# Sums of normalised activations for the seven-product multiplication: from GpSimd to VectorE

## The chip, the core and the metric

The kernel runs on one core of a Trainium2 chip. The metric is the device time of one execution in microseconds (us). In the profile PE is TensorE's matmuls, PEld its weight loads, DVE is VectorE, ACT is ScalarE, POOL is GpSimd and SP the engine that issues most of the DMAs.

## The reference

A decoder trunk of two residual layers over x of 512 tokens by 1024 features, in fp32, with a final norm. Each layer has an attention part and then a gated feed-forward part with a causal convolution of width 3. The change lies in the feed-forward part, which runs in both layers:

```
h = rmsnorm(x, ffn_norm[layer])            # x * rsqrt(mean(x*x) + 1e-6) * g
a, b = jnp.split(h @ w_in, 2, axis=-1)     # 1024 -> 2 x 2816
a = causal_conv3(a, conv_w) + conv_b
x = x + (jax.nn.silu(a) * b) @ w_out       # 2816 -> 1024
```

## The kernel before

Everything is kept transposed: features on the 128 partitions, 512 tokens along the free axis. X has 8 such tiles (NK = 8). To keep fp32 accuracy each operand is split in a high part (a cast to fp32r, by ACT) and a low part (the rest, by DVE), and a product is three matmuls: high x high, low x high, high x low. The names end in h or hi and l or lo (whi/wlo, xh/xl, sxh/sxl, gh/gl, b1h/b1l, t3h/t3l and so on).

`ffn(layer, nl, final)` computes the 22 chunks c of 128 hidden features. For each, a and b need 1024 x 128 weights times X. The first six chunks (PLAIN = 6) are done directly by `plain`: two units of 24 matmuls on 512 columns. They use x that is scaled by g but not yet by rstd; rstd is multiplied in at the evacuation, so that PE can start before the norm is known. The other sixteen chunks (`seven`) use a 2 x 2 block multiplication with seven products instead of eight, with the two halves of the tokens (LO, HI) and the two halves of the features (k and k + H, H = 4) as the blocks. That needs sums of blocks of the weights (`total`: p1, p2 and p4 on DVE, p3 on GpSimd) and sums of blocks of the normalised activations. The latter are made once per layer by `sums(k)` for k = 0 to 3, after rstd (root) is known, while PE works on the plain chunks. `sums(k)` does, in order: x[k] and x[k + 4] normalised on DVE; then four operations on half tiles of 128x256, s1 to s4, which fill d1 and d3 (two halves each); then the split of four operands into high and low parts, b1, b2, t1 (from d1) and t3 (from d3), a cast on ACT and a subtraction on DVE each. The last of these jobs, for all four k, are the list TJ, and every one of the seven products waits for all of TJ. In the profile x[k] has the tile name gh, and d1 and d3 have the name gl, because they are taken from the same buffers as the gated results GH and GL; the token "g" counts these ten buffers.

The outputs (`out(m, p)`) multiply the gated chunks of part p (PARTS: chunks 0 to 5, 6 to 11, 12 to 16, 17 to 21) with w_out for each of 8 tiles m and add to X[m].

The order of work on every engine is not written by hand: `add` gives a job to `Plan` with an engine, a planned cost, its dependencies, a priority (lower goes first) and buffer tokens that it takes and gives. `Plan.run` simulates the engines with these costs, picks at each step the job that can start first (priority decides among those that are ready), and emits the instructions in that order; each engine then works through its instructions in just that order. Priorities around the change: evacuations 1, convolution and gate 1.1, weight parts 1.2, weights of the outputs 1.3, `sums` 2 + 0.1 k; on PE, plain units and seven products 100 + c, outputs 200 + p. So the planned cost and the engine of one job can move the order of all that comes after it within the same feed-forward layer. Both layers get their own plan from the same code. Nearly all instructions carry line 88, the helper that records the order.

Of the kernel before, what the change touches and what calls it, by code (L numbers as in the profile page):

```python
# [39 lines left out]
class Fill:  # L40
# [5 lines left out]
    def add(self, *gens):  # L46
        self.q.extend([g, False] for g in gens)
# [122 lines left out]
def trunk(ctx, tc, A):  # L170
    nc = tc.nc
    inorder = [False]
    pe, act, dve, pool, sp = [Ordered(tc, e, inorder, e is nc.sync)
                              for e in (nc.tensor, nc.scalar, nc.vector, nc.gpsimd, nc.sync)]
# [946 lines left out]
    def ffn(layer, nl, final):  # L1121
# [7 lines left out]
        with ExitStack() as es:  # L1129
# [14 lines left out]
            def g_tile(t, dt=F32R):  # L1144
                return fp.tile([P, SEQ], dt, tag=t, bufs=10, name=t)

            def split(h, l, x, n, prio, *deps, take=(), give=()):

                j = add("ACT", 0.19 + 0.00085 * n, lambda: act.copy(h(), x()), *deps, prio=prio, take=take)
                return add("DVE", 0.16 + 0.00104 * n, lambda: dve.tensor_sub(l(), x(), h().bitcast(F32)), j, prio=prio, give=give)  # L1150
# [88 lines left out]
            def sums(k, root):  # L1239

                x = {}

                def norm(c):
                    x[c] = g_tile("gh", F32)
                    dve.scalar_tensor_tensor(x[c], X[c], ng[:, nl - 1, c:c + 1], rstd, op0=ALU.mult, op1=ALU.mult)
                    if c >= H:
                        x["d1"], x["d3"] = g_tile("gl", F32), g_tile("gl", F32)
                p = 2 + 0.1 * k
                j = add("DVE", 0.75, lambda: norm(k), root[0], prio=p, take=("g",))
                j = add("DVE", 0.75, lambda: norm(k + H), j, prio=p, take=("g",))  # L1250
                eng, e, cost = (pool, "POOL", 0.74) if True else (dve, "DVE", 0.42)
                s1 = add(e, cost, lambda: eng.tensor_sub(x["d1"][:, LO], x[k][:, LO], x[k][:, HI]), j, prio=p)
                s2 = add(e, cost, lambda: eng.tensor_add(x["d1"][:, HI], x[k + H][:, HI], x["d1"][:, LO]), s1, prio=p)
                s3 = add(e, cost, lambda: eng.tensor_sub(x["d3"][:, LO], x[k + H][:, HI], x[k][:, HI]), s2, prio=p)
                s4 = add(e, cost, lambda: eng.tensor_sub(x["d3"][:, HI], x["d1"][:, HI], x[k + H][:, LO]), s3, prio=p)
                part = lambda n, i: (lambda: B[n][i][:, k])
                a = split(part("b1", 0), part("b1", 1), lambda: x[k][:, LO], W, p, j, s4)
                b = split(part("b2", 0), part("b2", 1), lambda: x[k + H], SEQ, p, j, s4, give=("g",))
                c = split(part("t1", 0), part("t1", 1), lambda: x["d1"], SEQ, p, s2, s4)
                d = split(part("t3", 0), part("t3", 1), lambda: x["d3"], SEQ, p, s4, c, b, give=("g",))  # L1260
                TJ.extend((a, b, c, d))
# [137 lines left out]
            for c in range(PLAIN):  # L1399
                plain(c, root)  # L1400
                if c == 0:
                    for k in range(H):
                        sums(k, root)
# [277 lines left out]
```

## Time and profile before

| what | value |
|---|---|
| median of 3 runs | 1250.48 us (1249.95 to 1252.03) |
| the profiled execution | 1250.37 us, of which the span 1248.2 us |
| granted TensorE clock, mean | 0.995 |
| feed-forward part of the first layer | about 290 to 650 us of the span: plain chunks to 360.4, seven products to 611.9 |
| feed-forward part of the second layer | about 882 us to the end: plain chunks to 951.4, seven products to 1203 |

The span runs from the first to the last instruction in the trace of one execution; times in rows are us from its start unless marked ns. A matmul's shown duration overlaps with the next one's, so its cost is the step from one start to the next.

### The profile page before, as it was taken

The numbers are of one execution on the slowest core, as the hardware profiler recorded it, in microseconds if no ns is written. First come the engines' busy times: TensorE is split into PE (matmuls) and PEld (weight loads), VectorE is DVE, ScalarE is ACT, GpSimd is POOL, SyncE is SP. The second block draws the span as 40 slices with busy tenths as digits, with TensorE's granted clock in tenths as the row PEclk, the third lists the DMA queues.
The fourth block names the chain that finished last, engine by engine and source line by source line (L and its number), as shares of the span: only waits on it lengthen the run. The fifth ranks groups of instructions, "written<-read, shape, count | busy, mean of one in ns | idle before, by whom it ended". The sixth has DMA issues, their size and how long they took to land.

```text
span 1248.2 us, 19483 instructions
## 1 busy us (share of the span) xinstructions
PE 1223.1 (98%) x7484; PEld 1038.2 (83%) x7484; DVE 923.0 (74%) x1576; ACT 631.6 (51%) x1148; POOL 230.2 (18%) x272
## 2 busy tenths in 40 slices
PE   8999999999999999999999999999999999999997
PEld 5887866677889999999887878777788999999986
DVE  6668757658998799888762443444899889988875
ACT  6676537745554445444452664542555445444452
POOL 0000104413510001000030452310441000100011
PEclk9999999999999999999999999999999999999999
DMA  6314141012251342323233553312225124232421
GB/s 213 118 35 124 52 130 52 18 51 83 86 169 41 113 132 81 114 72 137 78 109 105 188 160 98 110 52 85 85 86 168 64 94 148 72 108 82 131 66 68
DMA packets 51420, 124.18 MB, mean 99 GB/s; under 512 B 6064, under 2 KB 17584, under 8 KB 51328
## 3 DMA queue, kind: packets, MB, share of 16 engines
q1 hardware_dynamic: 49808, 121.35, 30.0%
q10 hardware_dynamic: 1520, 1.59, 0.4%
q8 instruction: 59, 0.97, 0.3%
q14 instruction: 33, 0.27, 0.1%
HBM read 119.28 MB, written 2.13 MB: 97 GB/s over the span
## 4 chain that ended last, share of the span: by engine, by line
PE 88%; DVE 6%; ACT 1%; issue 1%; SPq 1%; DMA 1%; POOL 1%; DVEq 0%; ACTq 0%; POOLq 0%
PE mm L88 50%; PE s L88 20%; PE t L88 10%; PE o L88 7%; SPq L88 1%; DVE x L88 1%; DVE xl L88 1%; DVE wlo L88 1%; POOL e L88 1%; DVE e L88 1%; ACT whi L88 0%; DMA x<-x 0%; DVE sxl L88 0%; ACT xh L88 0%; DMA swp<-q 0%
## 5 line engine op out<-in xcount | busy, mean ns | idle before, releaser
L88 PE MATMUL mm<-xl,whi 128*128 128x512 f32 x424 | 166.2, 392 | 5.0 <-DVE xl L88 4.9
L88 PE MATMUL mm<-xh,whi 128*128 128x512 f32 x424 | 169.5, 400 | 1.4 <-ACT xh L88 1.4
L88 PE MATMUL mm<-xh,wlo 128*128 128x512 f32 x424 | 165.7, 391 | 1.1 <-DVE wlo L88 1.1
L88 DVE TENSOR_TENSOR wlo<-wraw,whi 128x1024 fp32r<-128x1024 f32 (+3 forms) x83 | 105.8, 1275 | 55.0 <-ACT whi L88 54.7
L88 ACT CAST whi<-wraw 128x1024 fp32r<-128x1024 f32 (+3 forms) x83 | 83.8, 1010 | 99.3 <-PE mm L88 73.8
L88 POOL TENSOR_TENSOR sr<-wraw,wb 128x512 f32<-128x512 f32 x32 | 47.4, 1481 | 462.8 <-DVE sr L88 288.1
L88 PE MATMUL mm<-gh,wlo 128*128 128x512 f32 x332 | 130.1, 392 | 0.0
L88 PE MATMUL mm<-gh,whi 128*128 128x512 f32 x332 | 130.0, 392 | 0.0
L88 PE MATMUL mm<-gl,whi 128*128 128x512 f32 x332 | 129.2, 389 | 0.0
L88 ACT CAST sxh<-sr 128x512 fp32r<-128x512 f32 x128 | 76.4, 617 | 83.5 <-DVE sr L88 54.2
L88 DVE TENSOR_TENSOR x<-x,mm 128x512 f32<-128x512 f32 (+2 forms) x104 | 70.0, 674 | 63.9 <-PE mm L88 63.5
L88 PEld LDWEIGHTS mm<-xl,whi 128*128 128x128 f32 x424 | 79.8, 188 | 24.6 <-DVE xl L88 7.5
L88 POOL TENSOR_SCALAR e<-e,dn 128x128 f32<-128x128 f32 (+3 forms) x128 | 72.3, 586 | 148.7 <-DVE dn L88 148.6
L88 PEld LDWEIGHTS mm<-xh,whi 128*128 128x128 f32 x424 | 79.9, 189 | 21.4 <-issue 3.3
L88 DVE TENSOR_TENSOR sxl<-sr,sxh 128x512 fp32r<-128x512 f32 x128 | 95.0, 760 | 2.7 <-ACT sxh L88 1.9
L88 PEld LDWEIGHTS mm<-xh,wlo 128*128 128x128 f32 x424 | 80.0, 189 | 18.1 <-DVE wlo L88 1.7
L88 ACT ACTIVATE tt<-a,conv 128x512 f32<-128x512 f32 x44 | 36.0, 817 | 114.5 <-DVE a L88 114.5
L88 ACT ACTIVATE e<-e,nm 128x256 f32<-128x256 f32 (+3 forms) x128 | 70.8, 556 | 43.9 <-DVE nm L88 40.9
L88 DVE SCALAR_TENSOR_TENSOR tt<-a,conv,tt 128x510 f32<-128x510 f32 x88 | 72.6, 826 | 8.4 <-ACT tt L88 7.2
L88 PEld LDWEIGHTS mm<-gl,whi 128*128 128x128 f32 x332 | 62.4, 188 | 13.3
L88 PE MATMUL s<-t3l,sxh 128*128 128x256 f32 x256 | 72.4, 283 | 0.0
L88 PE MATMUL s<-t3h,sxl 128*128 128x256 f32 x256 | 72.4, 283 | 0.0
(248 smaller groups left out, 3372.4 us busy)
## 6 DMA issues: line engine op xcount, KB each, us to landing
wraw<-wfi SPq DMA_DIRECT2D x56, 512.0 KB
wb<-wfi SPq DMA_DIRECT2D x32, 512.0 KB
wraw<-wu SPq DMA_DIRECT2D x31, 512.0 KB
wo<-wfo SPq DMA_DIRECT2D x32, 384.0 KB
wo<-wfo SPq DMA_DIRECT2D x28, 320.0 KB
wraw<-wo SPq DMA_DIRECT2D x16, 512.0 KB
wraw<-wv SPq DMA_DIRECT2D x10, 512.0 KB
cb<-cd SPq DMA_DIRECT2D x8, 512.0 KB
```

The lines of the kernel that those rows point to most:

```text
L88: r = f(*a, **k)
```

## The change

The engine variable that makes s1 to s4 in `sums` is GpSimd before and VectorE after; the planned cost of one goes from 0.74 to 0.42 us. The four operations, their operands, their dependencies and their priority stay. The function runs for four k in each of two layers, so 32 operations change their engine.

```
-                eng, e, cost = (pool, "POOL", 0.74) if True else (dve, "DVE", 0.42)
+                eng, e, cost = dve, "DVE", 0.42
                 s1 = add(e, cost, lambda: eng.tensor_sub(x["d1"][:, LO], x[k][:, LO], x[k][:, HI]), j, prio=p)
                 s2 = add(e, cost, lambda: eng.tensor_add(x["d1"][:, HI], x[k + H][:, HI], x["d1"][:, LO]), s1, prio=p)
                 s3 = add(e, cost, lambda: eng.tensor_sub(x["d3"][:, LO], x[k + H][:, HI], x[k][:, HI]), s2, prio=p)
```

The fourth operation, `s4`, follows in the same form.

## Rows read from the trace of the kernel before

**Rows 1.** The page: busy time, share of the span and instructions of each engine.
```profile
PE 1223.1 (98%) x7484; PEld 1038.2 (83%) x7484; DVE 923.0 (74%) x1576; ACT 631.6 (51%) x1148; POOL 230.2 (18%) x272
```

**Rows 2.** Windows: length, busy PE, PEld, DVE, ACT, POOL (instructions), clock, DMA share, GB/s.
```profile
290.00:360.38 70.38, 67.94 (x290) 55.02 (x289) 65.47 (x83) 38.17 (x57) 24.90 (x20) 0.98 0.33 109
360.38:611.90 251.52, 250.98 (x1736) 234.37 (x1735) 219.50 (x360) 115.14 (x195) 23.70 (x16) 1.00 0.30 99
...
882.10:951.37 69.27, 66.83 (x292) 54.18 (x290) 65.70 (x83) 38.25 (x57) 25.11 (x20) 1.00 0.34 111
951.37:1203.00 251.63, 251.39 (x1737) 234.61 (x1736) 220.13 (x362) 115.83 (x197) 23.70 (x16) 1.00 0.29 97
```

**Rows 3.** What PE waited for, whole span: us in total, times, longest us.
```profile
PE mm L88 <- DVE xl L88: 4.9, 2, 2.4
...
PE o L88 <- DVE sxl L88: 0.4, 1, 0.4
```

**Rows 4.** Groups by form on POOL, whole span: busy us, mean ns, idle before.
```profile
L88 POOL TENSOR_TENSOR gl<-gh 128x256 f32<-128x256 f32 x16 | 22.9, 1433 | 18.1 <-DVE gh L88 18.1
...
L88 POOL TENSOR_TENSOR gl<-gl,gh 128x256 f32<-128x256 f32 x8 | 10.6, 1319 | 0.0
L88 POOL TENSOR_TENSOR gl<-gh,gl 128x256 f32<-128x256 f32 x8 | 8.3, 1037 | 46.3 <-DVE gh L88 46.3
```

**Rows 5.** Timeline of POOL in the first layer: start us, duration us.
```profile
305.79 0.74 POOL L88 TENSOR_TENSOR gl<-gh 128x256 f32<-128x256 f32 x1 [9.47 <-DVE gh L88]
...
324.16 2.38 POOL L88 TENSOR_TENSOR gl<-gh 128x256 f32<-128x256 f32 x1
```

**Rows 6.** Groups by form on DVE between 304.3 and 357.25 us.
```profile
L88 DVE TENSOR_TENSOR wlo<-wraw,whi 128x1024 fp32r<-128x1024 f32 x9 | 11.7, 1303 | 0.0
...
L88 DVE SCALAR_TENSOR_TENSOR tt<-a,conv,tt 128x510 f32<-128x510 f32 x5 | 5.6, 1128 | 0.0
L88 DVE SCALAR_TENSOR_TENSOR tt<-a,conv,tt 128x511 f32<-128x511 f32 x5 | 5.2, 1037 | 0.2
...
L88 DVE TENSOR_TENSOR b1l<-gh,b1h 128x256 fp32r<-128x256 f32 x4 | 2.7, 684 | 0.0
```

**Rows 7.** Timeline of DVE in the first layer's plain stretch.
```profile
302.85 0.69 DVE L88 SCALAR_TENSOR_TENSOR rs_u<-rs_t,rs_u 128x512 f32<-128x512 f32 x1
303.58 0.69 DVE L88 SCALAR_TENSOR_TENSOR rstd<-rs_u,rstd 128x512 f32<-128x512 f32 x1
...
306.74 1.53 DVE L88 SCALAR_TENSOR_TENSOR tt<-a,conv,tt 128x510 f32<-128x510 f32 x2
...
317.53 0.41 DVE L88 TENSOR_TENSOR b1l<-gh,b1h 128x256 fp32r<-128x256 f32 x1
317.87 0.68 DVE L88 TENSOR_TENSOR b2l<-gh,b2h 128x512 fp32r<-128x512 f32 x1
318.47 0.68 DVE L88 TENSOR_TENSOR b<-mm,rstd 128x512 f32<-128x512 f32 x1
...
325.86 2.38 DVE L88 SCALAR_TENSOR_TENSOR tt<-a,conv,tt 128x510 f32<-128x510 f32 x2
...
342.80 1.22 DVE L88 TENSOR_TENSOR wlo<-wraw,whi 128x1024 fp32r<-128x1024 f32 x1
...
356.54 0.68 DVE L88 TENSOR_TENSOR t3l<-gl,t3h 128x512 fp32r<-128x512 f32 x1
```

**Rows 8.** Timeline of PE: a plain unit's first matmul, and the first of the seven products.
```profile
344.01 0.39 PE L88 MATMUL mm<-xh,whi 128*128 128x512 f32 x1
...
360.38 0.28 PE L88 MATMUL s<-b1h,sxh 128*128 128x256 f32 x1
```

**Rows 9.** Timeline of DVE in the second layer: the last part made from the sums.
```profile
947.60 0.68 DVE L88 TENSOR_TENSOR t3l<-gl,t3h 128x512 fp32r<-128x512 f32 x1
```

**Rows 10.** The chain that ended last, in order of time: start us, us, what.
```profile
398.85 15.67 PE mm L88 x69
```

**Rows 11.** Windows, the 10 us in that block; columns as in rows 2.
```profile
400.00:410.00 10.00, 10.00 (x46) 8.29 (x45) 6.83 (x10) 3.87 (x6) 0.00 (x0) 1.00 0.51 184
```

More of the change, by code (lines that the diff above doesn't have):

```diff
@@ L1250, in sums @@
                 j = add("DVE", 0.75, lambda: norm(k + H), j, prio=p, take=("g",))
-                eng, e, cost = (pool, "POOL", 0.74) if True else (dve, "DVE", 0.42)
+                eng, e, cost = dve, "DVE", 0.42
                 s1 = add(e, cost, lambda: eng.tensor_sub(x["d1"][:, LO], x[k][:, LO], x[k][:, HI]), j, prio=p)
```

## The prediction

> **What bounds the kernel now.** I read the profile from the whole to the place of the change. The busy line comes first: PE is busy for 1223.1 of the 1248.2 us of span, DVE 74%, POOL 18% [rows 1]. The cut by stages says the same of both feed-forward layers: in the stretch with the plain products PE is busy for 67.94 of 70.38 us, in the stretch of the seven products for 250.98 of 251.52, and the second layer repeats it with 66.83 of 69.27 and 251.39 of 251.63 [rows 2]. In the plain stretch DVE is almost as full (65.47 of 70.38), so both engines have to be watched. The list of what PE waited for names what is not covered: 4.9 us in two waits for xl, and 0.4 us for sxl [rows 3]. The xl wait lies before rstd exists, and no sum can start before rstd, so this change cannot touch it. What is left for it to win is the missing PE time of the two later stretches: 251.52 - 250.98 = 0.54 and 251.63 - 251.39 = 0.24 us [rows 2], together 0.8 us or 0.06% of the time. So the question is only whether the change makes PE wait.
>
> **What is removed.** 32 GpSimd instructions on 128x256 tiles, 16 in each layer: in the trace d1 and d3 are called gl and the x tiles gh. They took 22.9 + 10.6 + 8.3 = 41.8 us in all [rows 4]. GpSimd sits idle around them, so its own time buys nothing. What matters is what they do to DVE. The first of them, run with little DVE work beside it, took 0.74 us; another took 2.38 [rows 5]. DVE's instructions beside them are stretched too: a pair of convolution taps took 1.53 us in one place and 2.38 beside the sums, b1l 0.41 and 0.68 on average [rows 6, 7]. I price this from the means of the plain stretch, against an undisturbed one: taps 5 x (1.128 - 0.75) + 5 x (1.037 - 0.75) = 3.3 us, b1l 4 x (0.684 - 0.41) = 1.1, wlo 9 x (1.303 - 1.22) = 0.75 [rows 6, 7], where 0.75 is about half of the undisturbed pair and 1.22 a wlo with no sum beside it. That is 5.2 us of DVE given back in each layer. Bounds: nothing if the stretching has another cause, 5.2 if all of it is GpSimd's. I take 5.2, because the stretched rows lie exactly where a sum runs.
>
> The Trainium skill, page "SBUF — State Buffer", section "Who interferes with whom", says that a DVE instruction with two SBUF inputs and a GpSimd instruction that reads SBUF take an exclusive lock, so that the later one is fully blocked. Taken to its end, each of the 16 sums would hold DVE off for its whole 0.74 us, an estimate of 11.8 us per layer instead of the 5.2 of the rows; DVE would then come out 5.9 us lighter, not heavier, and the wait of the first rival below could not arise. The trace agrees in kind (both sides of an overlapping pair are lengthened) but not in that amount.
>
> **What is added.** The same 32 operations on DVE. A 256-column fp32 subtraction there is busy for 0.41 us, but the next instruction starts 0.34 us after it (317.53 to 317.87); at 512 columns the step is 0.60 (317.87 to 318.47), and 0.73 where the next one reads the result (302.85 to 303.58), 0.13 more [rows 7]. In a group of four only the second reads what the one before it wrote, so a group costs 4 x 0.34 + 0.13 = 1.49 us and four groups 6.0 us per layer. Bounds: 16 x 0.34 = 5.4 (others in between) and 16 x 0.47 = 7.5 (all dependent). Net on DVE: 6.0 - 5.2 = +0.8 us per layer, between +0.2 (5.4 - 5.2) and +7.5 (no relief).
>
> **What covers it.** The last thing that the products need from the sums is t3l of group 3. It ends at 356.54 + 0.68 = 357.22, and the first of the seven products starts at 360.38 [rows 7, 8]: 3.2 us of room. In the second layer it ends at 947.60 + 0.68 = 948.28 against 951.37: 3.1 us [rows 2, 9]. So +0.8 fits. If that cover were gone, each further us on DVE would be a us on PE, twice. There is a narrower place: wlo of one plain unit ends at 342.80 + 1.22 = 344.02, just as the unit starts at 344.01 (its second matmul is the first to read it) [rows 7, 8]. DVE's backlog there comes from the stretched taps and b1l, 0.85 + 0.27 us in a group, which go away; and the new operations have the lowest urgency (2 + 0.1k against 1 to 1.2 for evacuations, gates and weights), so the planner puts them behind what PE waits for. I expect this margin to grow.
>
> **The order moves too.** The planner knows neither the contention nor the 0.34. It now sees 16 x 0.42 = 6.7 us more on DVE, where it saw GpSimd doing 16 x 0.74 in parallel. Its DVE is nearly full there already. By its own costs one plain chunk asks of DVE 2 x 0.69 + 2 x 0.72 + 2 x 0.69 + 2 x 1.22 = 6.6 us and one group of sums 4.0, against 16 x 0.685 = 10.96 us on PE. With 1.7 us more per group the four groups don't fit any more, so I expect up to some 7 us of sums to be planned behind the last plain unit, and the seven products later by as much or more, since fresh evacuations and weight parts go first. Does PE then starve? It has other work: the output products of part 0 (8 x 18 matmuls) need only the six plain chunks, and today 69 of them run as one block of 15.7 us at 398.85, while DVE is only 6.83 of 10 us busy [rows 10, 11]. The planner takes whatever PE can do first, so it will pull output products ahead and shorten that block. The DVE gaps there let its backlog drain, and behind that block both layers should run as before. PE does the same work in another order: I price it at +0.1 to +0.2 us per layer for small gaps, like the 0.4 us that today's order leaves.
>
> **Sum.** Profiled execution: 1250.37 us (span 1248.2, the rest lies around it). Removed from PE's path 0, added 0, gaps of a new order 2 x 0.15 = 0.3: 1250.7. The median of the runs shown, 1250.48, lies 0.1 above the profiled one, so no further shift is made.
>
> **Rivals.**
> (1) *The first product waits for the sums* (other side, slower). Place: t3l of group 3 before the first seven product. If the sums are planned late but PE's queue still has the products first, and the relief doesn't come, DVE is 6.0 us later and the room is 3.2: 2.8 us per layer, 5.6 in all. A wait of PE also lowers its clock: both layers have one of the two xl waits, and the first layer's plain stretch has a granted clock of 0.98 on average and is 1.1 us longer than the second's at 1.00, 70.38 against 69.27 [rows 2, 3]. With 1.1 to 2.2 for that: about 1258. It decides from 3.1 us of net DVE delay on; I have 0.8, and the output products stand ready. Chance 0.10.
> (2) *The new order leaves gaps.* The output products are spent early, and later in the seven stage (DVE 219.50 of 251.52 us busy [rows 2]) PE meets a product whose parts aren't ready with nothing to fill in. Both layers have the same order, so any gap counts twice: 1.5 to 2.5 us per layer gives 1253.5 to 1255.5. For it: DVE has only 13% to spare, in lumps. Against it: a 15.7 us block to draw on, and actual steps (0.60) below the planned 0.69. Chance 0.14.
> (3) *DVE sets the pace.* The whole 6.0 us lands on PE's time in both layers: 1262. For it speaks DVE's 93% in the plain stretch, against it PE's 97%. Chance 0.02. The Trainium skill ("Perfetto Trace Analysis", section "Optimizing Scalar/DVE Operations") supports this one: it allows moving work off a saturated DVE, even to GpSimd, and this change goes the other way; but it adds that a move between those two may not help, as they share a port.
> (4) *Faster.* All of today's gaps close: 0.8 us, 1249.7, still no change that can be told. More than 0.2% would need a gain that no row shows. Chance 0.04.
> That the change doesn't do what it says is no rival: all 16 calls go through one engine variable.
>
> **How the numbers follow.** No change to speak of: 0.70, with 1249.3 to 1252.5 as its own range. 0.2% is 2.5 us, about what a measurement of this kernel tells from nothing. Slower by more: 0.10 + 0.14 + 0.02 = 0.26. Faster by more: 0.04. The range runs from 1248.8 (all gaps closed, and the spread of the runs) up into the second rival, to 1255.5; about 0.12 is left above and 0.03 below.
>
> **What would show it.** GpSimd's 32 gl rows gone and its busy time down by some 42 us; 32 new DVE rows at about 0.41 us; tap pairs at 1.53, b1l at 0.41 and wlo at 1.22 throughout the plain stretch; DVE's busy time within 3 us of before; output products (mm<-gh) ahead of the first seven product, and the block of 69 shorter; PE's busy share in the four stretches as before. I am wrong if PE shows a wait for t3l or t3h at the first product, or more than 1 us of new waits for sxl, b or wlo in the seven stage.

## The result, and the profile after

The changed kernel takes 1258.22 us (median of four runs, 1255.93 to 1259.78); the kernel before, run beside it, 1250.47 (1249.95 to 1252.03). The ratio is 1.0056, with a 95% interval from 1.0042 to 1.007: slower by 0.56%, which lies above the range given. The profiled execution took 1255.93 us, the lowest of the four, with a span of 1254.1; so 5.9 us of span are to be explained from rows, and the medians differ by 2 us more, which is taken up below.

The page, busy time of each engine, after:

```profile
PE 1223.2 (98%) x7484; PEld 1036.6 (83%) x7484; DVE 929.0 (74%) x1608; ACT 631.3 (50%) x1148; POOL 184.9 (15%) x240
```

Against [rows 1] the 32 instructions have moved: POOL went from 272 to 240 instructions and from 230.2 to 184.9 us, DVE from 1576 to 1608 and from 923.0 to 929.0. PE does the same 1223 us. The span is longer only because PE stands idle for longer. The windows say where (same columns as [rows 2]; the first four answer to it):

```profile
290.00:360.38 70.38, 67.94 (x297) 55.12 (x297) 64.57 (x93) 37.01 (x54) 4.50 (x4) 1.00 0.32 109
360.38:611.90 251.52, 249.23 (x1714) 232.00 (x1713) 223.16 (x366) 115.98 (x198) 22.13 (x16) 1.00 0.29 98
882.10:951.37 69.27, 66.82 (x293) 54.47 (x292) 63.55 (x91) 37.09 (x55) 5.82 (x5) 1.00 0.34 118
951.37:1203.00 251.63, 249.34 (x1704) 231.46 (x1703) 223.43 (x366) 116.32 (x199) 21.83 (x16) 1.00 0.29 96
...
611.90:650.00 38.10, 37.54 (x177) 30.89 (x176) 25.29 (x35) 21.12 (x30) 10.99 (x8) 1.00 0.32 92
```

PE's idle time in the plain stretches is what it was (2.44 and 2.45 us). In the stretch behind them it was 0.54 and 0.24 us and is now 251.52 - 249.23 = 2.29 and 251.63 - 249.34 = 2.29. In the last window above, the end of the first layer, it is 38.10 - 37.54 = 0.56, where the kernel before had none (38.10 of 38.10). The list of PE's waits gives names to the loss (us in total, times, longest):

```profile
PE mm L88 <- DVE xl L88: 4.9, 2, 2.5
PE mm L88 <- DVE wlo L88: 4.0, 3, 1.4
...
PE mm L88 <- ACT gh L88: 1.9, 2, 1.4
PE mm L88 <- DVE gl L88: 1.4, 2, 0.7
```

The wait for xl is the old one [rows 3], the one for sxl is gone. The kernel before had 1.1 us for wlo, in one wait outside the feed-forward parts, and none for gh or gl. So the new waits are 4.0 - 1.1 + 1.9 + 1.4 - 0.4 = 5.8 us, against 5.9 of span: nearly the whole difference. Each of the three new kinds appears once in each layer. PE's timeline in the first layer (start us, duration us) shows them and what stands around them; [rows 8] is its counterpart:

```profile
358.81 0.39 PE L88 MATMUL mm<-gh,whi 128*128 128x512 f32 x1
...
363.73 0.50 PE L88 MATMUL mm<-gl,whi 128*128 128x512 f32 x1 [0.71 <-DVE gl L88]
...
370.01 0.50 PE L88 MATMUL mm<-gh,wlo 128*128 128x512 f32 x1 [1.45 <-DVE wlo L88]
...
377.41 0.28 PE L88 MATMUL s<-b1h,sxh 128*128 128x256 f32 x1
...
620.00 0.50 PE L88 MATMUL mm<-gh,whi 128*128 128x512 f32 x1 [0.56 <-ACT gh L88]
```

Here mm<-gh and mm<-gl are output products of part 0 (gh and gl are now the gated results, wlo a low part of w_out). They begin at 358.81, right behind the last plain unit, and the first of the seven products comes at 377.41 instead of 360.38. In the 18.6 us between them PE waits twice for inputs of the output products themselves. At the layer's end it waits for gh, the gated result of the last chunk. The second layer repeats the pattern, with a longer wait at its end:

```profile
957.83 0.50 PE L88 MATMUL mm<-gl,whi 128*128 128x512 f32 x1 [0.71 <-DVE gl L88]
...
964.11 0.50 PE L88 MATMUL mm<-gh,wlo 128*128 128x512 f32 x1 [1.45 <-DVE wlo L88]
...
1214.90 0.50 PE L88 MATMUL mm<-gh,whi 128*128 128x512 f32 x1 [1.36 <-ACT gh L88]
```

What the medians have beyond the 5.9 us is found in a place where the change does nothing, the 20 us around the norm (windows, the kernel before and then the changed one, in two fences):

```profile
290.00:310.00 20.00, 17.56 (x68) 13.35 (x67) 16.01 (x18) 9.82 (x14) 5.19 (x5) 0.91 0.16 53
```

```profile
290.00:310.00 20.00, 17.56 (x75) 13.66 (x75) 17.06 (x20) 10.40 (x15) 4.50 (x4) 1.00 0.21 66
```

Behind the wait for xl the granted clock was 0.91 in the profiled execution of before and 1.00 in that of the changed kernel, and 68 matmuls ran there instead of 75. Seven matmuls at their step of 0.23 us are 1.6 us, by which the plain work ends sooner: output products start at 358.81, where before had its first product at 360.38. With an equal clock the two spans would differ by 5.9 + 1.6 = 7.5 us, near the 7.75 of the medians. Besides the waits' 5.8 us that includes longer steps around each of them (behind a wait 0.50 us are shown and not 0.39). Counted by starts in PE's timeline, from the last plain unit to the layer's last output product, and taking every step that is 0.1 us or more above the usual one (0.23 us at 512 columns, 0.12 at 256), the excess is 4.4 us in the first layer and 5.2 in the second. The kernel before, counted in the same way, has 1.2 and 1.0: 7.4 us less.

Why the inputs are late stands in DVE's timeline of the same place, the counterpart of [rows 7]:

```profile
354.18 0.74 DVE L88 SCALAR_TENSOR_TENSOR gh<-x,ng,rstd 128x512 f32<-128x512 f32 x1
...
361.89 1.78 DVE L88 TENSOR_TENSOR gl<-b,gh 128x512 fp32r<-128x512 f32 x1
363.60 1.28 DVE L88 TENSOR_TENSOR sxl<-sr,sxh 128x512 fp32r<-128x512 f32 x2
...
369.01 0.95 DVE L88 TENSOR_TENSOR wlo<-wo,whi 128x768 fp32r<-128x768 f32 x1
369.88 0.68 DVE L88 TENSOR_TENSOR t3l<-gl,t3h 128x512 fp32r<-128x512 f32 x1
370.48 0.42 DVE L88 TENSOR_TENSOR gl<-gh 128x256 f32<-128x256 f32 x1
...
371.61 0.42 DVE L88 TENSOR_TENSOR gl<-gl,gh 128x256 f32<-128x256 f32 x1
...
375.42 0.68 DVE L88 TENSOR_TENSOR t3l<-gl,t3h 128x512 fp32r<-128x512 f32 x1
```

The last normalisation is made at 354.18, as the last chunk still runs, but the sums of group 3 (370.48 to 371.61) and their last split (to 376.10, in the kernel before 357.22) come 16 us later in DVE's planned order, behind gates, parts of seven-product weights (sxl) and parts of output weights (wlo). The same queue makes all that the output products need. So the work that PE was given to bridge DVE's backlog hangs on DVE's backlog: gl<-b,gh is done at 363.67 and PE starts at 363.73; wlo is done at 369.96 and PE starts at 370.01.

### The profile page after: what moved, and what is told of

Its sections match the earlier page's. It is cut to its first block, busy times and chain, and to the rows that moved or that the text cites. A ratio compares the mean times of both kernels' runs of the same rounds, so it can differ in the third digit from the quotient of the medians.

```text
span 1254.1 us, 19482 instructions
## 1 busy us (share of the span) xinstructions
PE 1223.2 (98%) x7484; PEld 1036.6 (83%) x7484; DVE 929.0 (74%) x1608; ACT 631.3 (50%) x1148; POOL 184.9 (15%) x240
## 4 chain that ended last, share of the span: by engine, by line
PE 64%; DVE 4%; ACT 1%; issue 1%; POOL 0%; DMA 0%; DVEq 0%; ACTq 0%; SPq 0%; POOLq 0%
PE mm L88 34%; PE s L88 17%; PE t L88 9%; PE o L88 5%; DVE sxl L88 1%; DVE x L88 1%; DVE wlo L88 1%; DVE xl L88 0%; DVE tt L88 0%; POOL e L88 0%; DVE b L88 0%; DVE sr L88 0%; DMA wraw<-wfo 0%; ACT sxh L88 0%; ACT L212 0%
## 5 line engine op out<-in xcount | busy, mean ns | idle before, releaser
L88 POOL TENSOR_TENSOR sr<-wraw,wb 128x512 f32<-128x512 f32 x32 | 44.0, 1374 | 579.4 <-DVE sr L88 299.4
L88 PEld LDWEIGHTS mm<-gh,wlo 128*128 128x128 f32 x332 | 62.6, 188 | 15.0 <-DVE wlo L88 4.4
L88 DVE SCALAR_TENSOR_TENSOR tt<-a,conv,tt 128x510 f32<-128x510 f32 x88 | 67.7, 769 | 8.7 <-ACT tt L88 7.3
L88 PEld LDWEIGHTS mm<-gh,whi 128*128 128x128 f32 x332 | 62.6, 188 | 13.8 <-ACT gh L88 2.8
```

What stands on the lines that cost most here:

```text
L88: r = f(*a, **k)
```

## The experiments

Theory A: the order of the planned queues made the loss, not the work that DVE got. Theory B, the rival: the added work on DVE, or what is left of the contention, made it. An engine and a cost are given to the planner separately from the engine that the instruction runs on, so the two can be taken apart. Every ratio is to the kernel before, run beside the experiment: its median was 1251.32 us for experiments 1 to 8 and 1250.54 for 9 and 10.

**1. The operations on VectorE, in the order of before.** GpSimd's cost and name are left to the planner.

```
-                eng, e, cost = dve, "DVE", 0.42
+                eng, e, cost = dve, "POOL", 0.74
```

> The 32 operations run on VectorE as in the changed kernel, but the planner is told that they are GpSimd's at 0.74 us, so PE's order is exactly that of the kernel before and only VectorE's queue has the 32 operations put in. Theory A (the new order costs the time): 1250.5 us, between 1249 and 1252; PE's waits for wlo, gh and gl at the output products are gone, DVE's stretched taps are back at 1.53 us a pair. Theory B (VectorE's own added time, 6.0 us a layer, costs it): it stays near 1258.

Measured: 1249.61 us (1248.37 to 1254.21), ratio to before 0.9989 [0.9978, 1.0001]. The page, and from the list of PE's waits the one for wlo:

```profile
PE 1220.7 (98%) x7484; PEld 1036.7 (83%) x7484; DVE 920.5 (74%) x1608; ACT 632.9 (51%) x1148; POOL 191.8 (15%) x240
```

```profile
PE mm L88 <- DVE wlo L88: 1.0, 1, 1.0
```

DVE's and PE's timelines, the last split and the first of the seven products:

```profile
355.16 0.69 DVE L88 TENSOR_TENSOR t3l<-gl,t3h 128x512 fp32r<-128x512 f32 x1
...
358.70 0.28 PE L88 MATMUL s<-b1h,sxh 128*128 128x256 f32 x1
```

And two groups by form on DVE between 303.4 and 357.25 us, the counterparts of [rows 6]:

```profile
L88 DVE TENSOR_TENSOR wlo<-wraw,whi 128x1024 fp32r<-128x1024 f32 x9 | 11.0, 1220 | 0.0
L88 DVE SCALAR_TENSOR_TENSOR tt<-a,conv,tt 128x511 f32<-128x511 f32 x6 | 4.5, 751 | 0.2
```

The whole loss is gone with the order. DVE has the same 1608 instructions as in the changed kernel, yet is busy for 2.5 us less than before, with 32 instructions more. The last split ends at 355.85 and the first product starts at 358.70: 2.85 us of room, where before had 3.16; in the second layer 2.88 against 3.09. So the move leaves DVE 0.2 to 0.3 us later at that place. Theory A holds, and B falls.

**2. The reverse: the operations on GpSimd, in the new order.**

```
+                eng, e, cost = pool, "DVE", 0.42
```

> The opposite: the operations run on GpSimd as before, but the planner is told that they are VectorE's at 0.42 us, so the order is that of the changed kernel. Theory A: 1257 to 1260 us, as slow as the change, with the same PE waits around 362 to 370 us of the span. Theory B: 1250.5, as VectorE has nothing added.

Measured: 1262.17 us (1261.52 to 1264.13), ratio 1.0088 [1.0072, 1.0103]. The same waits at the same places, and the one for wlo longer:

```profile
PE mm L88 <- DVE wlo L88: 7.2, 3, 3.1
...
PE mm L88 <- ACT gh L88: 2.1, 2, 1.5
...
PE mm L88 <- DVE gl L88: 1.4, 2, 0.7
```

The order alone, with nothing moved to DVE, does the harm. In that order the operations are better off on VectorE, by 3 to 4 us: 1262.17 is 10.9 us above the kernel before that ran beside it, the changed kernel 7.75.

**3 and 4. One group of sums moved, and two groups.** The rest stays on GpSimd.

```
+                eng, e, cost = (dve, "DVE", 0.42) if k < 1 else (pool, "POOL", 0.74)
```

and `k < 2` in the fourth.

> Only the sums of k = 0 go to VectorE (8 of 32 operations), planned at 0.42. Theory A: with one group the sums are still planned to be done before the plain chunks end, PE's planned order has no waits, so 1250.5 us (1249 to 1252). Theory B: a quarter of the loss, 1252.4.

> The sums of k = 0 and 1 go to VectorE (16 of 32), planned at 0.42. Theory A: it is a threshold, not a rate; with two groups the last group already falls behind the work of the seven products in the plan, so the whole loss or more, 1256 to 1264 us. Theory B: half of the loss, 1254.3.

Measured: one group 1250.86 us, ratio 1.0001 [0.9988, 1.0014]; two groups 1263.64, ratio 1.01 [1.0082, 1.0118]. Half of the change costs more than all of it, a quarter nothing. A cost that comes with the load would grow with the number of operations; this is a threshold at which the planner's queues turn over. By the planner's own costs, PE's idle time in a feed-forward layer comes out at 0 us before, 0 with one group, 7.6 with two and 5.1 with four: planned costs, no times of the chip, but in the order that the chip shows. With two groups waits for sxl, inside the seven products, come in:

```profile
PE mm L88 <- DVE wlo L88: 4.1, 4, 1.4
PE o L88 <- DVE sxl L88: 3.1, 6, 1.2
```

**5. The early output products held back.** Is their early start itself the harm, or only cover for something late? In the changed kernel they wait for all sums.

```
-                    j = add("PE", 0.685, step, wj, j, GJ[c0 + k], prio=200 + p, ...
+                    j = add("PE", 0.685, step, wj, j, GJ[c0 + k], *TJ, prio=200 + p, ...
```

> The changed kernel, but the output products may start only after the last sum is split, so that PE can't put them ahead of the first of the seven products. If the early output products are what costs the time, this brings it back towards 1250. If they are only a poor cover for sums that come some 17 us late (377.41 against 360.38 for the first product), PE now stands idle for most of that in both layers: 1275 to 1292 us.

Measured: 1276.18 us (1274.64 to 1276.91), ratio 1.0195 [1.0177, 1.0214]. PE now waits for the sums, in both layers:

```profile
PE s L88 <- ACT b1h L88: 11.2, 2, 5.6
PE s L88 <- DVE b1l L88: 7.7, 2, 3.9
```

The output products are cover: without them the late sums cost 1276.18 - 1251.32 = 25 us instead of 8. They don't cover all. A part of the 25 us is a lower clock behind the long waits: between 358 and 378 us of the span the granted clock was 0.74, and the mean of these runs is 0.987 to 0.989, against 0.995 to 0.996 in those of the changed kernel.

**6. The sums made twice.** The kernel of experiment 1 with each of the 32 operations issued two times, to see how much more DVE could take in the good order.

```
+                twice = lambda f: lambda: (f(), f())
+                s1 = add(e, cost, twice(lambda: eng.tensor_sub(...)), j, prio=p)
```

and so for s2 to s4.

> The run with the planner's old order, but each of the 32 operations is done twice in a row on VectorE, which the planner isn't told. This adds 16 x 0.34 to 16 x 0.42 us, about 6 us a layer, to VectorE and nothing else. The room at the first product was 2.85 us in that run (355.85 to 358.70). If the room was read rightly, PE now waits about 3 us in each layer before the first product: 1255 to 1258 us. If VectorE's time sets the pace, 12 us are added: 1262. If it is hidden anywhere, 1250.

Measured: 1263.5 us (1262.02 to 1264.9), ratio 1.0095 [1.0076, 1.0114]. The time that I expected, 1255 to 1258, was missed; what I had written for the case that VectorE sets the pace, 1262, came near. The second of each pair comes dearer than I priced it: in DVE's timeline a pair is busy for 0.88 us where one operation took 0.42, so 32 x 0.46 = 14.7 us of DVE were added, and the time rose by 1263.5 - 1249.61 = 13.9. I had put the first wait at the first product, behind 2.85 us of room. It came in the plain units, in the list of waits and in PE's timeline:

```profile
PE mm L88 <- DVE wlo L88: 9.7, 12, 1.5
```

```profile
328.34 0.50 PE L88 MATMUL mm<-xh,wlo 128*128 128x512 f32 x1 [1.52 <-DVE wlo L88]
```

So VectorE had next to no room left in the plain stretch. The move in experiment 1 was free because the relief from GpSimd paid for it, not because DVE had time to spare. Of theory B this much is left: 14.7 us more on DVE cost nearly their full time.

**7. The output weights made earlier.** In the changed kernel the weight parts of the outputs, which were late at 369.96, go ahead of convolution and gate (1.1), behind evacuations (1).

```
-                q = 1.3 + 0.01 * p + 0.001 * m
+                q = 1.05 + 0.001 * p + 0.0001 * m
```

> The changed kernel with the output products' weights more urgent (priority 1.05 instead of 1.3), so ahead of the weight sums and parts of the seven products on ACT and VectorE. If the change's loss is made of waits of the output products for wlo (1.61 us a layer) and of the end of each layer (0.72 and 1.52 us), part of it should go: 1254 to 1257 us, and the wait for gh at the end of each layer disappears. The sums stay as late as in the changed kernel.

Measured: 1259.58 us (1258.65 to 1259.99), ratio 1.0065 [1.0044, 1.0086]; no gain over the changed kernel, and my expectation was missed. The wait for gh at the layer's end is gone, but others took its place, one of them for the high parts from ACT. The list of waits, and the 10 us of the first layer that hold a wait of each kind (window, columns as in [rows 2]):

```profile
PE mm L88 <- DVE wlo L88: 4.2, 3, 1.6
PE mm L88 <- ACT whi L88: 2.5, 2, 1.2
```

```profile
366.00:376.00 10.00, 7.19 (x24) 5.23 (x23) 8.70 (x15) 5.51 (x10) 0.00 (x0) 0.83 0.38 126
```

One due time moved doesn't mend the order. That the whole backlog behind the plain units is too much for DVE fits this, but the run doesn't show it.

**8 and 9. A version that beats both.** The largest of PE's waits in the profile of before is the one for xl [rows 3]. The low weight part of the layer's second plain unit stands ahead of the last xl on DVE; here it is issued behind them, in the kernel of experiment 1 (8) and in the kernel before (9).

```
+    xl_done = []
...
+            self.plan.add("DVE", 0.75, lambda: xl_done.append(dve.scalar_tensor_tensor(XL[m], ...).ins), a, prio=4)
...
-            first = [weights(A["wfi"][layer, u], [P, NK, P]) for u in range(2)]
+            first = [weights(A["wfi"][layer, u], [P, NK, P], after=xl_done[-1] if u else None) for u in range(2)]
...
+        if after is not None:
+            with tc.issue_after(after):
+                dve.tensor_sub(l, w, h.bitcast(F32))
+            return h, l
```

> A version that may beat both: the run with the planner's old order (sums on VectorE), and besides the wlo of a layer's second unit is issued after the last two xl on VectorE, because in every kernel so far PE waits 2.44 to 2.5 us for xl at the start of both layers while VectorE makes that wlo (2.08 us). Expected: the two xl waits fall to some 0.5 us, and PE's clock has less reason to drop behind them: 1244 to 1247.5 us. If PE then waits for the wlo instead, no change against 1249.6.

> The kernel before (sums on GpSimd, old order) with the last version's second edit alone: wlo of a layer's second unit after the last two xl. It tells what share of 1247.0 is due to the sums on VectorE. If they give nothing by themselves, 1247 us here too; if the 1.7 us that the sums with the old order seemed to gain are real, 1248.5.

Measured: 1246.96 us with the sums on VectorE, ratio 0.9964 [0.995, 0.9977]; 1247.14 with the sums on GpSimd, ratio 0.9972 [0.996, 0.9985]. In both the wait for xl falls from 5 us to this:

```profile
PE mm L88 <- DVE xl L88: 2.1, 4, 0.8
```

The gain is this edit's: 1250.54 - 1247.14 = 3.4 us over the kernel before, 1249.61 - 1246.96 = 2.7 over experiment 1. Between the two kernels no difference can be told: in a good order it doesn't matter to the time which of the two engines makes the sums.

**10. The change in the first layer alone.**

```
+                eng, e, cost = (dve, "DVE", 0.42) if nl == 2 else (pool, "POOL", 0.74)
```

> The change in the first feed-forward layer alone (16 operations); the second layer keeps GpSimd and its order. If each layer loses by its own order, about half of the loss: 1253 to 1256 us, with PE's waits at 363 and 370 us of the span there and none in the second layer.

Measured: 1252.27 us (1251.44 to 1254.6), ratio 1.0012 [1.0001, 1.0024], against 1250.54: 1.7 us, a little under what I expected and less than half of the 7.75 of both layers. The waits are those of the first layer of the changed kernel:

```profile
PE mm L88 <- DVE wlo L88: 2.5, 2, 1.4
...
PE mm L88 <- DVE gl L88: 0.7, 1, 0.7
PE mm L88 <- ACT gh L88: 0.6, 1, 0.6
```

Against before they add 2.5 - 1.1 + 0.7 + 0.6 = 2.7 us by the profile, 1 us more than the medians say. That would leave 7.75 - 1.7 = 6 us for the second layer alone. Its end does cost more (1.36 us against 0.56), but by the steps in PE's timeline above it loses 5.2 - 1.0 = 4.2 us and the first layer 3.2: how the loss is shared out between the layers is not settled to better than 2 us.

## Why the prediction was wrong

The step that failed is the last term of the sum: "PE does the same work in another order: I price it at +0.1 to +0.2 us per layer for small gaps". The new order was foreseen and came as written: sums planned behind the last plain unit, output products of part 0 pulled ahead of the seven; the block of 69 matmuls [rows 10] no longer stands at 398.85, and 69 stand at 358.81 instead. What it costs was not foreseen. The output products wait for their own low parts (gl, wlo), which DVE's late queue makes, and at the layer's end too few of them are left. It cost 5.8 us of waits in the profiled execution and 7.75 us by the medians, 3 to 4 us a layer: some twenty times the price. Point by point:

- "GpSimd sits idle around them, so its own time buys nothing", and the relief of DVE. Right. In experiment 1 taps are at 751 ns, wlo at 1220, as priced; the relief is about as large as the sums.
- "Net on DVE: +0.8 us per layer." Right in sign and about right in size: at the first product 0.2 to 0.3 us of room are lost in experiment 1, at the weights of the plain units 0 to 1.1. The Trainium skill, page "SBUF — State Buffer", section "Who interferes with whom", says that a DVE instruction with two SBUF inputs contends with a GpSimd instruction that reads SBUF, and calls this contention an exclusive lock. Taken to its end, as the prediction did, DVE would have come out 5.9 us lighter a layer; here it came out about even, so the amount is that of the rows.
- "I expect this margin to grow" (wlo in the plain stretch). Right in the changed kernel, for one of its two reasons. Before, wlo was ready at 344.02 and first read at 344.24; in the changed kernel that is 339.88 and 342.72, 2.8 us instead of 0.2, as these lines of DVE's and PE's timelines show:

```profile
338.66 1.22 DVE L88 TENSOR_TENSOR wlo<-wraw,whi 128x1024 fp32r<-128x1024 f32 x1
...
342.72 0.39 PE L88 MATMUL mm<-xh,wlo 128*128 128x512 f32 x1
```

  It is the planner, which put the sums behind, that widened it. The relief alone did not: in experiment 1 it is 0.24 us (342.37 to 342.61), and experiment 6 put the first waits at such places as soon as DVE got more.
- "So +0.8 fits", the cover of the first product. Right for the old order, by experiment 1, but in the new order this room no longer exists: the last split ends at 376.10, and the first product follows at 377.41. I had expected "up to some 7 us of sums" behind the last plain unit and the products later "by as much or more"; the last split came 19 us later and the first product 17.
- "Does PE then starve? It has other work." Half right. Experiment 5 shows the other work to be worth some 17 us, lower clock included (25 us lost without it, 8 with it). I counted that work (144 matmuls) and not its inputs: low parts of output weights and gated results come from the same DVE queue whose backlog they were to cover. I had even noted that "fresh evacuations and weight parts go first", which is what filled DVE from 354 to 370 us.
- "Behind that block both layers should run as before." Wrong at the end, where PE waits for gh of the last chunk. Output products could have stood there and had been spent: behind the last of the seven products of the first layer 3 x 46 = 138 output matmuls were left in the kernel before, and 3 x 42 = 126 in the changed one. One of the three forms of output matmul in that stretch, before (611.78 to 643.2) and after (615.17 to 644.9):

```profile
L88 PE MATMUL mm<-gh,whi 128*128 128x512 f32 x46 | 17.9, 389 | 0.0
```

```profile
L88 PE MATMUL mm<-gh,whi 128*128 128x512 f32 x42 | 16.5, 392 | 0.6 <-ACT gh L88 0.6
```

  In the first layer of all runs the wait goes with this count: with 126 matmuls it is there (the changed kernel, experiments 2, 5 and 10), with 135 (experiment 4), 138 (the kernel before and the experiments with its order or with one group) and 144 (experiment 7) it is not. Experiment 5 holds the products of part 0 until the sums are done and still has 126, so it is the new order as a whole and not their early start that spends them. By the planner's costs, too, 1.5 of the 5.1 idle us lie at this place.
- The rivals. Rival 2, gaps of the new order, came nearest, with 1.5 to 2.5 us a layer a price that was too low. It had the wait at the layer's end, with output products spent and nothing to fill in, but not the waits for gl and wlo: those are of the early output products themselves, ahead of the seven. Of the signs of being wrong, new waits for wlo of more than 1 us behind the plain stretch came, with 2.9 us. Rival 1 had the number, 1258, with a mechanism that did not occur: no wait for t3l or t3h at the first product. Rival 3, VectorE as the pace, is what experiment 6 made, at 1263.5 against its 1262.

I listed the new order's gaps as a rival and gave them 0.14, since I took a planner that "takes whatever PE can do first" for one whose plan would hold no idle time. By its own costs it held 5.1 us a layer, which could have been worked out from the costs in the code.

Open stays the share of each layer.

## What to carry to other kernels

Where a planner or a fixed order feeds in-order queues, a change of engine is two changes: work moves, and the order of every engine may turn over. Run them apart, by moving the instruction under the old plan and by changing the plan under the old engine; here the first cost nothing and the second everything. And when other work is to cover a late engine, follow the inputs of that work back: here cover that was fed by the late engine covered only part.

## What the runs showed of the hardware

- VectorE and GpSimd beside each other lengthen both. GpSimd's sums took 0.74 us with little on DVE and up to 2.38 beside it [rows 5]. Without the sums on GpSimd, DVE's taps took 751 and 748 ns instead of 1037 and 1128, and b1l 420 instead of 684 [rows 6]. As much as moving 32 instructions onto DVE cost it, it got back: 920.5 us busy against 923.0. It is still seen where another GpSimd instruction is left: gl<-b,gh of 512 columns took 1.78 us at 361.89 in the changed kernel, beside a sum of weights (sr) on GpSimd from 361.32 to 363.12, and 0.69 at 310.29 and 318.95.
- A wait of PE can lower its clock behind it, and it does not always. After the 1.45 us wait in the changed kernel the second step is 0.23 us again. In experiment 2, behind a 3.08 us wait for the same weight part, PE ran at the lower of its two levels (1.2 and not 2.4 GHz) for six matmuls, as this timeline shows: steps of 0.43 us between starts, and then 0.23. Behind the same wait in the second layer of that run (3.07 us, at 970.86) the steps are 0.23 us again from the second on; the granted clock of 10 us around them is 0.83 in the first layer (366 to 376) and 1.00 in the second (964 to 974). Behind the two waits of experiment 7 the granted clock was 0.83 in the 10 us shown.

```profile
372.52 0.79 PE L88 MATMUL mm<-gh,wlo 128*128 128x512 f32 x1 [3.08 <-DVE wlo L88]
373.12 0.63 PE L88 MATMUL mm<-gl,whi 128*128 128x512 f32 x1
373.54 0.63 PE L88 MATMUL mm<-gh,whi 128*128 128x512 f32 x1
...
375.60 0.39 PE L88 MATMUL mm<-gl,whi 128*128 128x512 f32 x1
375.83 0.40 PE L88 MATMUL mm<-gh,whi 128*128 128x512 f32 x1
```

- The spread of one kernel's runs goes with the mean granted clock, and the 20 us around the norm show one place of it (0.91 against 1.00 after the same wait of 2.4 to 2.5 us). Of the 23 runs of the kernel before beside experiments 1 to 4, the four at 0.997 or above took 1249.48 to 1250.06 us, the twelve at 0.994 1251.32 to 1254.71. It is a tendency: of the 13 beside experiments 5 to 8, the three at 0.997 or above took 1248.52 to 1250.31, the seven at 0.993 or 0.994 1249.95 to 1254.02.
